# Seven query products of a cross-attention in another order, with one more accumulation bank and earlier bank copies

## The chip, the cores and the metric

The kernel runs on one NeuronCore of a Trainium2 chip. The metric is the device time of one execution in microseconds. Its engines are named as in the profile: PE (TensorE, matrix products), PEld (TensorE's weight loads), ACT (ScalarE), DVE (VectorE), POOL (GpSimd) and SP (SyncE, which here only issues transfers). Each engine works through its own queue in order; semaphores tie the queues together.

## The reference

One layer of a streaming encoder over 512 tokens with 1024 features, in fp32: a combined input projection, forgetting attention and a gated linear recurrence side by side, an output projection, cross-attention to 256 memory tokens, a squared-ReLU MLP, and a final norm. The change lies in the cross-attention:

```python
def memory_cross_attention(h, mem_n, w_q, w_kv, w_o):
    b_, s_, _ = h.shape
    m_ = mem_n.shape[1]
    q = (h @ w_q).reshape(b_, s_, X_HEADS, X_HEAD_DIM)
    kv = mem_n @ w_kv
    k, v = jnp.split(kv, 2, axis=-1)
    ...
    s = jnp.einsum('bshd,bmhd->bhsm', q, k).astype(jnp.float32) / math.sqrt(X_HEAD_DIM)
    p = jax.nn.softmax(s, axis=-1)
    o = jnp.einsum('bhsm,bmhd->bshd', p.astype(v.dtype), v).reshape(b_, s_, D_MODEL)
    return o @ w_o
```

There are four heads of 256 features. `h` is normalised before (its row scale is applied inside the softmax), and `w_q` is 1024 x 1024.

## The kernel before

**Precision.** Every fp32 operand of a large product is split into a high part that TensorE takes in one pass (dtype fp32r) and the rest as a low part. A product is then three matmuls: high x high, high x low and low x high. Splitting 128 x 1024 weights is one copy on ACT (line 190, `wh.. <- wr..`) and one subtraction on DVE (line 194, `wl.. <- wr..,wh..`). The raw weights come by transfers on SP's queue (line 216 for panels, line 322 for query products).

**Seven products.** For heads 2 and 3 (g = 1) the query product q = x @ w_q, with x cut into two halves of features and two halves of tokens, and w_q into two halves of features and two of columns, is not done as eight block products but as seven on sums of blocks, after Winograd's variant of Strassen's scheme. They are named 1 to 7; the sums of weight blocks (5, 6, 7) are made earlier by accumulating transfers into DRAM (`wsq`), the sums of activation blocks (5, 6, 3, 7) on ACT and DVE (`x1_sums`, line 1421 on; `x1_last` makes 3 in the buffers that 6 has used). Product 4's raw weights are those of product 6 plus a block that a transfer on POOL's queue adds in place, once product 6's weights are split (line 325).

Each product is 24 matmuls of 128 x 256 on two row blocks (lines 1485 to 1487). They are accumulated in PSUM banks: U takes products 1, 6, 7 and 4, one after the other. A copy of U after product 1 starts bank V, to which product 2 is added: this is head 2, tokens 0 to 255 (`xq..20`). Product 5 goes to bank Y and from there to SBUF (`y5s`, tile `xy`). A copy of U after product 6 replaces Y, to which product 3 is added. U after product 7 plus `y5s` is head 3, second half (`xt7`); U after product 4 is head 2, second half; Y after product 3 plus `y5s` is head 3, first half (`xt3`). `q_out` splits a result in high (`xqh`, ACT, line 1466) and low (`xql`, DVE, lines 1468 and 1470).

**Banks.** `mm(...)` takes a bank from a pool of three (`mmp`); a new tile takes a bank that is free first, and its first writer waits until all readers of the old tile are done. The weight parts rotate through four buffers each (`whp`, `wlp`), so a split waits until the matmuls on the buffer's previous weights are done.

**Order.** PE's order is that of the program text: `fill` is a list of generators, from which pieces are taken between the steps of the softmax of each head (`x_scores`: scores `xs`, maximum `xm`, exponent `xp` on ACT line 1528, division on DVE line 1531; `x_T_`: transposes `xpt`; `x_out`: outputs `xo`). ACT and DVE are ordered by a scheduler, by priority: text order, moved ahead by `ahead(n)` (`tc.high_priority`); weight splits are given out with `PW = -20`, bank copies with none. The lines that set it:

```python
    P1, P2, P3, P4, PW = 20, 20, 20, 10, -20
    ...
    QORDER = [(1, name) for name in "1256743"]
    ...
        if h == 1:
            for g, name in QORDER[:-1]:
                fill.add(q_product(g, name), f"q{g}{name}")
        if h == 2:
            fill.add(q_product(1, "3"), "q13")
    ...
        if h < 2:
            fill.until(("xq1", "q14")[h])
```

The order of the names in `QORDER` also sets the order in which their weights are loaded and split. After the second scores of head 1 a piece of this list runs up to the transposes of head 1; the rest, through product 4, runs before the outputs of head 1; product 3 runs among the scores of head 2.

Of the kernel before, what the change touches and what calls it, by code (L numbers as in the profile page):

```python
# [9 lines left out]
F32 = mybir.dt.float32  # L10
R = mybir.dt.float32r
U8 = mybir.dt.uint8
AF = mybir.ActivationFunctionType
ALU = mybir.AluOpType
AX = mybir.AxisListType

P = 128
# [4 lines left out]
M = 256  # L22
# [10 lines left out]
P1, P2, P3, P4, PW = 20, 20, 20, 10, -20  # L33
# [13 lines left out]
def emit(  # L47
# [22 lines left out]
    te, ve, ac, gp = nc.tensor, nc.vector, nc.scalar, nc.gpsimd  # L70
# [32 lines left out]
    def q2(name):  # L103
        return q2p.tile([P, S], R, tag="q2", name=name)
# [4 lines left out]
    def t2(name, dt=F32, shape=(S,)):  # L109
        return t2p.tile([P] + list(shape), dt, tag="t2", name=name)  # L110
# [6 lines left out]
    def mm(name, shape=(S,)):  # L117
        return mmp.tile([P] + list(shape), F32, tag="mm", name=name)
# [4 lines left out]
    def sc(name, shape=(S,)):  # L123
        return scp.tile([P] + list(shape), F32, tag="sc", name=name)
# [4 lines left out]
    def f(a):  # L129
        return a.bitcast(F32)  # L130


    def panel(w, n0):
        return [(slice(0, WT), w[:, n0 : n0 + WT].rearrange("(k p) n -> p k n", p=P))]
# [31 lines left out]
        specs.append(panel(w_out, j * WT))  # L166
    for j in range(2):
        specs.append(panel(w_xq, j * WT))
    QORDER = [(1, name) for name in "1256743"]
    QFIRST = len(specs)  # L170
    specs += [lambda g=g, n=n: q_unit(g, n) for g, n in QORDER]
    for j in range(4):
# [125 lines left out]
    def parts_of(i):  # L298
        return 1 if QFIRST <= i < QFIRST + len(QORDER) else 2

    q_raw = {}

    def q_unit(g, name):
        hi, lo = new_parts([UK, WT], f"q{g}{name}")
        stream.append(([hi], [lo]))
        if name == "4":
            raw = q_raw.pop(g)
        else:
            if name == "6":
                raw = q_raw[g] = s4([UK, WT], f"wrq{g}{name}")  # L310
            else:
                state["halves"] += 1
                if state["halves"] % 3 == 0:
                    raw = t4(f"wrq{g}{name}")
                else:
                    raw = wrp.tile([P, D], F32, tag="wr", name=f"wrq{g}{name}", padded_shape=[P, UK * UW])
                raw = raw.rearrange("p (k n) -> p k n", k=UK)
            if name in SUMS:
                src = wsum["q", g, name]
            else:  # L320
                src = block_q(g, {"1": "00", "2": "10", "3": "11"}[name])
            nc.sync.dma_start(raw, src)
        jobs = [split_of(hi, lo, raw)]
        if name == "6":
            jobs.append(lambda: tc.keep_in_program_order(gp.dma_start(raw, block_q(g, "10"), accum_op=ALU.add)))
        return jobs

    def next_panel():
        while len(stream) < len(specs) and sum(parts_of(i) for i in range(state["used"], len(stream) + 1)) <= 4:
            for split in load_next():  # L330
                with ahead(PW):
                    split()
        r = stream[state["used"]]
        state["used"] += 1
        return r
# [51 lines left out]
    def ahead(n):  # L387

        return tc.high_priority(offset=n) if n else nullcontext()
# [396 lines left out]
    for hp in range(2):  # L786
# [8 lines left out]
        for j in range(2):  # L795
            h = 2 * hp + j
            ps = mm(f"gq{h}")
# [52 lines left out]
    U, W = [], []  # L850
# [112 lines left out]
    for li, m in enumerate(mlev):  # L963
# [10 lines left out]
        for hp in range(2):  # L974
# [3 lines left out]
            ps = sc(f"lv{hp}{m}", (NT, 2, w))  # L978
# [305 lines left out]
    for n in range(len(pairs) + 2):  # L1284
        if n < len(pairs):
            p, tb = pairs[n]
# [120 lines left out]
    xq, xps, xpr, xpT = {h: {} for h in range(4)}, {}, {}, {}  # L1407
# [50 lines left out]
    qbank, y5s = {}, {}  # L1458

    def q_out(h, tp, src, sign):  # L1460
        def half(part):
            name = f"xq{part}{h}{tp}"
            return q2(name).rearrange("p (i n) -> p i n", i=2) if h % 2 == 0 else t2(name, R, (2, M))

        a, b = half("h"), half("l")
        ac.activation(a, src, AF.Copy, scale=sign)
        if sign > 0:
            ve.tensor_tensor(b, src, f(a), ALU.subtract)
        else:
            ve.scalar_tensor_tensor(b, src, sign, f(a), op0=ALU.mult, op1=ALU.subtract)  # L1470
        xq[h][tp] = [(a[:, i, :], b[:, i, :]) for i in range(2)]

    def q_product(g, name):
        b = {"5": "Y", "3": "Y", "2": "V"}.get(name, "U")
        if (g, b) not in qbank:
            qbank[g, b] = mm(f"xq{b}{g}").rearrange("p (i n) -> p i n", i=2)
            if b == "V":
                ac.activation(qbank[g, b], qbank[g, "U"], AF.Copy)
        ps = qbank[g, b]
        (whi,), (wlo,) = next_panel()  # L1480
        xh, xl = x1s[name]
        for k in range(UK):
            for i in range(2):
                ws, begin = slice(i * P, (i + 1) * P), name in "15" and k == 0 and i == 0
                te.matmul(ps[:, i, :], whi[:, k, ws], xh[:, k, :], start=begin, stop=False, skip_group_check=True)
                te.matmul(ps[:, i, :], whi[:, k, ws], xl[:, k, :], start=False, stop=False, skip_group_check=True)
                at = te.matmul(ps[:, i, :], wlo[:, k, ws], xh[:, k, :], start=False, stop=k == UK - 1, skip_group_check=True)
            yield presum.tick(6 * WT / 2400, at)
        if name == "2":
            q_out(2 * g, 0, ps, 1.0)  # L1490
        elif name == "4":
            q_out(2 * g, 1, ps, 1.0)
        elif name == "5":
            y5s[g] = t2(f"xy5{g}", F32, (2, M))
            ac.activation(y5s[g], ps, AF.Copy)
        elif name == "6":
            ac.activation(qbank[g, "Y"], ps, AF.Copy)
            x1_last()
        elif name in "73":
            t = t2(f"xt{name}{g}", F32, (2, M))  # L1500
            ve.tensor_tensor(t, ps, y5s[g], ALU.add)
            q_out(2 * g + 1, 1 if name == "7" else 0, t, -1.0)
# [73 lines left out]
    for h in range(4):  # L1576
# [5 lines that stand above are left out]
            x2_hi, x2_lo = act_tile("x2_hi"), act_tile("x2_lo")  # L1582
            early, rest = residual(o_hi, o_lo, g_ff, x2_hi, x2_lo, "xw", None, range(KC), 2, to_tok, first_hooks, True)
            fill.add(early())
        if h == 3:
            fill.until("q13")
        x_scores(h, 0)
        fill.run(X1)
        x_scores(h, 1)
        fill.run(X2 + X3)  # L1590
        x_T_(h, 0)
        x_T_(h, 1)
        pth, ptl = s4([2, S], f"pth{h}", R), s4([2, S], f"ptl{h}", R)
        for mc in range(2):
            ac.activation(pth[:, mc, :], xpT[h][mc], AF.Copy)
            ve.tensor_tensor(ptl[:, mc, :], xpT[h][mc], f(pth[:, mc, :]), ALU.subtract)
        if h < 2:
            fill.until(("xq1", "q14")[h])
        else:
            fill.run(X4)  # L1600
        x_out(h, pth, ptl)
# [599 lines left out]
```

## Time and profile before

| what | value |
|---|---|
| runs | 753.63, 755.44, 759.96 us (median 755.44) |
| profiled execution | 755.39 us |
| its span, first to last instruction | 753.6 us |
| mean granted clock of TensorE | 0.997 |
| products 1 (end) to 4 of heads 2 and 3 | 343.96 to 366.40 us in the span |

In the profile, times are in microseconds from the span's start. A timeline row gives start, duration, engine, line, operation, output <- inputs, size, and in brackets the idle time of the engine before it with the instruction that ended it (its releaser). The durations of matmuls overlap their successors, so distances between starts are what counts. A row of the view of waits reads: who waited <- for whom, total, times, longest. A row of the view of windows gives the stretch, its length, then the busy time of PE, PEld, DVE, ACT and POOL with counts of instructions, the granted clock of TensorE, the DMA share and GB/s. A row on transfers ends with the KB of each and the time from issue to landing.

### The profile page before, as it was taken

The numbers are of one execution on the slowest core, as the hardware profiler recorded it, in microseconds if no ns is written. First come the engines' busy times: TensorE is split into PE (matmuls) and PEld (weight loads), VectorE is DVE, ScalarE is ACT, GpSimd is POOL, SyncE is SP. The second block draws the span as 40 slices with busy tenths as digits, with TensorE's granted clock in tenths as the row PEclk, the third lists the DMA queues.
The fourth block names the chain that finished last, engine by engine and source line by source line (L and its number), as shares of the span: only waits on it lengthen the run. The fifth ranks groups of instructions, "written<-read, shape, count | busy, mean of one in ns | idle before, by whom it ended". The sixth has DMA issues, their size and how long they took to land.

```text
span 753.6 us, 12520 instructions
## 1 busy us (share of the span) xinstructions
PE 740.1 (98%) x4629; PEld 648.6 (86%) x4629; DVE 584.5 (78%) x918; ACT 470.8 (62%) x786; POOL 219.1 (29%) x294
## 2 busy tenths in 40 slices
PE   9999999999999999998899999999999999999996
PEld 6888888898888888888887899898989899998985
DVE  5877996677788867964656799978878787878796
ACT  5965776566666733444544589766675757574864
POOL 7225942442443347531111213111111111100024
PEclk9999999999999999999999999999999999999999
DMA  8787999847946999986857798989898998977452
GB/s 251 233 219 195 252 304 341 250 168 246 346 165 197 296 297 242 211 186 109 196 112 167 119 263 221 254 218 242 204 245 224 241 235 218 245 204 229 135 113 112
DMA packets 115263, 163.94 MB, mean 218 GB/s; under 512 B 6481, under 2 KB 76922, under 8 KB 115202
## 3 DMA queue, kind: packets, MB, share of 16 engines
q1 hardware_dynamic: 86978, 117.24, 47.4%
q0 software_dynamic: 28064, 45.64, 34.4%
q8 instruction: 36, 0.59, 0.3%
q10 hardware_dynamic: 160, 0.27, 0.1%
q14 instruction: 25, 0.20, 0.1%
HBM read 157.87 MB, written 54.54 MB: 282 GB/s over the span
## 4 chain that ended last, share of the span: by engine, by line
PE 88%; DMA 4%; DVE 4%; issue 2%; ACT 2%; POOL 0%; POOLq 0%; DVEq 0%; ACTq 0%; SPq 0%
PE uU L1776 4%; PE uU L1778 4%; PE uU L1777 4%; PE U L1934 4%; PE U L1935 4%; PE U L1936 4%; PE uY L1778 2%; PE uY L1777 2%; PE uY L1776 2%; PE xk L1189 2%; PE wo L352 2%; PE wo L354 2%; PE Y L1934 2%; PE Y L1936 2%; PE Y L1935 2%; PE wo L353 2%
## 5 line engine op out<-in xcount | busy, mean ns | idle before, releaser
L194 DVE TENSOR_TENSOR wlu<-wru,whu 128x1024 fp32r<-128x1024 f32 x53 | 63.9, 1221 | 25.8 <-ACT whu L190 25.6
L190 ACT ACTIVATE whu<-wru 128x1024 fp32r<-128x1024 f32 x53 | 55.7, 1059 | 41.5 <-PE U L1936 16.8
L194 DVE TENSOR_TENSOR wld<-wrd,whd 128x1024 fp32r<-128x1024 f32 x56 | 68.2, 1221 | 13.8 <-ACT whd L190 13.6
L190 ACT ACTIVATE whd<-wrd 128x1024 fp32r<-128x1024 f32 x56 | 59.0, 1054 | 14.6 <-PE uU L1777 7.2
L1934 PE MATMUL U<-whd,hb 128*128 128x512 f32 x120 | 46.8, 390 | 0.0
L1935 PE MATMUL U<-wld,hb 128*128 128x512 f32 x120 | 46.8, 390 | 0.0
L1936 PE MATMUL U<-whd,hb 128*128 128x512 f32 x120 | 46.7, 389 | 0.0
L1776 PE MATMUL uU<-xs_hi,whu 128*128 128x256 f32 x128 | 36.3, 284 | 0.0
L1778 PE MATMUL uU<-x_hi,wlu 128*128 128x256 f32 x128 | 36.2, 283 | 0.0
L1776 PE MATMUL uY<-xs_hi,whu 128*128 128x256 f32 x128 | 36.2, 283 | 0.0
L1777 PE MATMUL uY<-xs_lo,whu 128*128 128x256 f32 x128 | 36.2, 283 | 0.0
L1778 PE MATMUL uY<-xs_hi,wlu 128*128 128x256 f32 x128 | 36.2, 283 | 0.0
L1777 PE MATMUL uU<-x_lo,whu 128*128 128x256 f32 x128 | 36.2, 283 | 0.0
L1777 PE MATMUL uU<-xs_lo,whu 128*128 128x256 f32 x128 | 36.2, 283 | 0.0
L1778 PE MATMUL uU<-xs_hi,wlu 128*128 128x256 f32 x128 | 36.2, 283 | 0.0
L1776 PE MATMUL uU<-x_hi,whu 128*128 128x256 f32 x128 | 36.2, 283 | 0.0
L1210 POOL TENSOR_SCALAR bi<-nF,Ft 128x128 f32<-128x128 f32 (+3 forms) x32 | 20.5, 649 | 52.4 <-PE pt L1246 30.9
L1672 POOL DMA_DIRECT2D wrd<-in_w_dram x8 | 9.7, 1213 | 83.4 <-DVE wld L194 76.3
L551 POOL DMA_DIRECT2D wsd<-in_w_dram x16 | 17.4, 1089 | 55.0 <-PE xw L354 13.4
L1672 POOL DMA_DIRECT2D wru<-in_w_dram x7 | 9.2, 1320 | 80.0 <-DVE wlu L194 80.0
L551 POOL DMA_DIRECT2D wsu<-in_w_dram x14 | 17.6, 1257 | 41.5 <-PE xw L354 18.5
L1936 PEld LDWEIGHTS U<-whd,hb 128*128 128x128 f32 x120 | 22.5, 188 | 4.8
(1028 smaller groups left out, 2726.3 us busy)
## 6 DMA issues: line engine op xcount, KB each, us to landing
wru<-in_w_dram SPq DMA_DIRECT2D x25, 512.0 KB, 6.2
wsd<-in_w_dram SPq DMA_DIRECT2D x24, 512.0 KB, 7.3
wrd<-in_w_dram SPq DMA_DIRECT2D x24, 512.0 KB, 8.0
wrd<-wsd SPq DMA_DIRECT2D x24, 512.0 KB, 4.2
wsu<-in_w_dram SPq DMA_DIRECT2D x21, 512.0 KB, 7.0
wru<-wsu SPq DMA_DIRECT2D x21, 512.0 KB, 4.8
wsd<-in_w_dram POOLq DMA_DIRECT2D x16, 512.0 KB, 7.6
wsu<-in_w_dram POOLq DMA_DIRECT2D x14, 512.0 KB, 7.8
```

The source lines that it names most:

```text
L190: at = ac.activation(hi, raw, AF.Copy)
L194: at_lo = ve.tensor_tensor(lo, raw, f(hi), ALU.subtract)
L352: te.matmul(ps, wh, hi, start=n_ == 0 and not begun, stop=False)
L551: yield gp.dma_start(wsum[kind, g, name], src, accum_op=ALU.add, **more)
L1210: gp.tensor_scalar(bi[:, 0:n], fF[h][:, 0:n], -1.0, Ft[:, tb, h : h + 1], op0=ALU.mult, op1=ALU.add)
L1672: tc.keep_in_program_order(gp.dma_start(box[0], block(g, "10"), accum_op=ALU.add))
L1776: te.matmul(ps[:, i, :], whi[:, k, ws], xh[:, k, :], start=begin, stop=False, skip_group_check=True)
L1777: te.matmul(ps[:, i, :], whi[:, k, ws], xl[:, k, :], start=False, stop=False, skip_group_check=True)
L1778: at = te.matmul(ps[:, i, :], wlo[:, k, ws], xh[:, k, :], start=False, stop=k == UK - 1, skip_group_check=True)
L1934: te.matmul(ps, hi, whi[:, k, :], start=begin, stop=False, skip_group_check=True)
L1935: te.matmul(ps, hi, wlo[:, k, :], start=False, stop=False, skip_group_check=True)
L1936: at = te.matmul(ps, lo, whi[:, k, :], start=False, stop=k == 1, skip_group_check=True)
```

## The change

The seven products run in the order 1, 5, 6, 2, 7, 4, 3 in place of 1, 2, 5, 6, 7, 4, 3. The copy of U that starts V is given out right behind product 1, with priority `P1`, and not when product 2 begins; the copy of U into Y gets the same priority. Product 4 starts a bank Z of its own (its first matmul overwrites); its result is put together from a copy of U in SBUF (`xt4`, a new activation) and an addition on DVE (new).

```diff
-    QORDER = [(1, name) for name in "1256743"]
+    QORDER = [(1, name) for name in "1562743"]
...
     def q_product(g, name):
-        b = {"5": "Y", "3": "Y", "2": "V"}.get(name, "U")
-        if (g, b) not in qbank:
-            qbank[g, b] = mm(f"xq{b}{g}").rearrange("p (i n) -> p i n", i=2)
-            if b == "V":
-                ac.activation(qbank[g, b], qbank[g, "U"], AF.Copy)
-        ps = qbank[g, b]
+        b = {"5": "Y", "3": "Y", "2": "V", "4": "Z"}.get(name, "U")
+
+        def bank(b):
+            qbank[b] = mm(f"xq{b}{g}").rearrange("p (i n) -> p i n", i=2)
+
+        if b not in qbank:
+            bank(b)
+        ps = qbank[b]
         (whi,), (wlo,) = next_panel()
         xh, xl = x1s[name]
         for k in range(UK):
             for i in range(2):
-                ws, begin = slice(i * P, (i + 1) * P), name in "15" and k == 0 and i == 0
+                ws, begin = slice(i * P, (i + 1) * P), name in "154" and k == 0 and i == 0
...
             yield presum.tick(6 * WT / 2400, at)
-        if name == "2":
+        if name == "1":
+            bank("V")
+            with ahead(P1):
+                ac.activation(qbank["V"], ps, AF.Copy)
+        elif name == "2":
             q_out(2 * g, 0, ps, 1.0)
         elif name == "4":
-            q_out(2 * g, 1, ps, 1.0)
+            t = t2(f"xt4{g}", F32, (2, M))
+            ac.activation(t, qbank["U"], AF.Copy)
+            ve.tensor_tensor(t, ps, t, ALU.add)
+            q_out(2 * g, 1, t, 1.0)
         elif name == "5":
             y5s[g] = t2(f"xy5{g}", F32, (2, M))
             ac.activation(y5s[g], ps, AF.Copy)
         elif name == "6":
-            ac.activation(qbank[g, "Y"], ps, AF.Copy)
+            with ahead(P1):
+                ac.activation(qbank["Y"], ps, AF.Copy)
             x1_last()
```

PE has the same instructions; the products stand in the new order, and the eight transposes of head 1 (`xpt1`) stand behind product 5, where they stood behind product 2. What the scheduler made of ACT and DVE is read from the built programs. In the names, the two digits of a query product's tiles are g and the product (`whq17`: high part of the weights of product 7); in `xp11`, `xs11` and `pth1` they are head and half of the tokens.

ACT, around the end of product 1, before:

```order
L190 ACTIVATE whq16_3923<-wrq16_3925 128x1024
L1551 ACTIVATE o_hi_3631<-xo0_3874 128x512
L1551 ACTIVATE o_hi_3631<-xo1_3883 128x512
L1528 ACTIVATE xp10_3910,xd10_3909<-xs10_3892,xn10_3907,r0_435 128x256 x2
L190 ACTIVATE whq17_3980<-wrq17_3982 128x1024
L1528 ACTIVATE xp11_3966,xd11_3965<-xs11_3948,xn11_3963,r0_435 128x256 x2
L1478 ACTIVATE xqV1_3978<-xqU1_3916 128x512
L190 ACTIVATE whq14_4032<-wrq16_3925 128x1024
```

ACT, the same place, in the change:

```order
L190 ACTIVATE whq16_3917<-wrq16_3919 128x1024
L1561 ACTIVATE o_hi_3631<-xo0_3874 128x512
L190 ACTIVATE whq12_3924<-wrq12_3926 128x1024
L1561 ACTIVATE o_hi_3631<-xo1_3883 128x512
L1538 ACTIVATE xp10_3910,xd10_3909<-xs10_3892,xn10_3907,r0_435 128x256 x2
L190 ACTIVATE whq17_3981<-wrq17_3983 128x1024
L1494 ACTIVATE xqV1_3978<-xqU1_3916 128x512
L1538 ACTIVATE xp11_3966,xd11_3965<-xs11_3948,xn11_3963,r0_435 128x256 x2
L190 ACTIVATE whq14_4030<-wrq16_3919 128x1024
```

The copy into V moved ahead of one softmax step, and stays behind the split of product 7. The split of product 2 now stands between the two output copies; the split of product 5 took its earlier place.

ACT, from the split of product 4 on, before:

```order
L190 ACTIVATE whq14_4032<-wrq16_3925 128x1024
L1466 ACTIVATE xqh20_4027<-xqV1_3978 128x512
L1595 ACTIVATE pth1_4021<-xpt10_4011 128x512
L1595 ACTIVATE pth1_4021<-xpt11_4012 128x512
L190 ACTIVATE whq13_4062<-wrq13_4064 128x1024
L1495 ACTIVATE xy51_4060<-xqY1_4031 128x512
L190 ACTIVATE wh38a_4130<-wr38a_4132 128x1024
L1497 ACTIVATE xqY1_4031<-xqU1_3916 128x512
L1425 ACTIVATE o_hi_3631<-xdif_3469 128x1024
```

ACT, the same place, in the change:

```order
L190 ACTIVATE whq14_4030<-wrq16_3919 128x1024
L1504 ACTIVATE xy51_4028<-xqY1_3980 128x512
L1605 ACTIVATE pth1_4022<-xpt10_4012 128x512
L1605 ACTIVATE pth1_4022<-xpt11_4013 128x512
L190 ACTIVATE whq13_4065<-wrq13_4067 128x1024
L1507 ACTIVATE xqY1_3980<-xqU1_3916 128x512
L1425 ACTIVATE o_hi_3631<-xdif_3469 128x1024
L190 ACTIVATE wh38a_4131<-wr38a_4133 128x1024
L1466 ACTIVATE xqh20_4096<-xqV1_3978 128x512
L190 ACTIVATE wh38b_4135<-wr38b_4137 128x1024
L1466 ACTIVATE xqh31_4126<-xt71_4124 128x512
L1499 ACTIVATE xt41_4168<-xqU1_3916 128x512
```

The copy into Y stands behind the split of product 3, and ahead of that of the first output panel (`wh38a`); V's high half (`xqh20`) moved behind both. The last row is the new copy.

DVE, at product 7, in the change (before, the low half `xql20` stood directly ahead of product 3's `wlq13`, and there was no `xt41`):

```order
L194 TENSOR_TENSOR wlq13_4066<-wrq13_4067,whq13_4065 128x1024
L1429 SCALAR_TENSOR_TENSOR o_lo_3632<-xdif_3469,o_hi_3631 128x1024
L194 TENSOR_TENSOR wl38a_4132<-wr38a_4133,wh38a_4131 128x1024
L1468 TENSOR_TENSOR xql20_4097<-xqV1_3978,xqh20_4096 128x512
L1511 TENSOR_TENSOR xt71_4124<-xqU1_3916,xy51_4028 128x512
L194 TENSOR_TENSOR wl38b_4136<-wr38b_4137,wh38b_4135 128x1024
L1470 SCALAR_TENSOR_TENSOR xql31_4127<-xt71_4124,xqh31_4126 128x512
L1500 TENSOR_TENSOR xt41_4168<-xqZ1_4130,xt41_4168 128x512
```

The low half of V, its last reader, moved behind two weight steps. In the built program Z has V's bank, and product 4's first matmul waits for DVE there. On SP's queue the loads of `wrq12` and `wrq15` change places; POOL's queue has the same order.

## The prediction

> **What bounds the kernel now.** I read the page first: busy time by engine and the chain that ended last.
>
> ```profile
> span 753.6 us, 12520 instructions
> PE 740.1 (98%) x4629; PEld 648.6 (86%) x4629; DVE 584.5 (78%) x918; ACT 470.8 (62%) x786; POOL 219.1 (29%) x294
> PE 88%; DMA 4%; DVE 4%; issue 2%; ACT 2%; POOL 0%; POOLq 0%; DVEq 0%; ACTq 0%; SPq 0%
> ```
>
> TensorE (PE) is busy for 98% of the span, so only two things can be won: moments when it waits, and moments when its clock is low. The view of waits, cut to PE, orders the first kind.
>
> ```profile
> PE xqV L1485 <- ACT xqV L1478: 2.6, 1, 2.6
> PE xqU L1485 <- ACT xqY L1497: 1.5, 1, 1.5
> PE warm L464 <- DVE ones L468: 1.3, 1, 1.3
> PE xqU L1485 <- DVE xt L1501: 0.8, 1, 0.8
> ```
>
> Three of the four longest waits lie in the seven query products of heads 2 and 3, which are what the change reorders. The timeline of PE there (start, duration, and in brackets the idle time before, with its releaser) gives their real price.
>
> ```profile
> 343.84 0.28 PE L1487 MATMUL xqU<-x_hi,wlq 128*128 128x256 f32 x1
> 346.73 0.47 PE L1485 MATMUL xqV<-x_hi,whq 128*128 128x256 f32 x1 [2.61 <-ACT xqV L1478]
> 351.20 1.03 PE L1540 MATMUL xpt<-ident,xp 128*128 128x128 f32 x8
> 352.00 0.36 PE L1485 MATMUL xqY<-o_hi,whq 128*128 128x256 f32 x1
> 354.94 0.28 PE L1485 MATMUL xqU<-o_hi,whq 128*128 128x256 f32 x1
> 357.70 0.28 PE L1487 MATMUL xqU<-o_hi,wlq 128*128 128x256 f32 x1
> 359.50 0.39 PE L1485 MATMUL xqU<-o_hi,whq 128*128 128x256 f32 x1 [1.51 <-ACT xqY L1497]
> 362.36 0.28 PE L1487 MATMUL xqU<-o_hi,wlq 128*128 128x256 f32 x1
> 363.42 0.39 PE L1485 MATMUL xqU<-x_hi,whq 128*128 128x256 f32 x1 [0.78 <-DVE xt L1501]
> 366.40 0.40 PE L1548 MATMUL xo<-pth,xvh 128*128 128x512 f32 x1
> ```
>
> Matmuls overlap, so I go by starts. A product is 24 matmuls; product 6, undisturbed, runs from 354.94 to 357.82 (its last start, 357.70, and one step of 0.12): 2.88 us. Against that, PE loses 2.77 us before product 2 (343.96 to 346.73), 1.68 us before product 7 (357.82 to 359.50) and 0.94 us before product 4 (362.48 to 363.42). And product 2 itself takes 346.73 to 351.20, 4.47 us, 1.59 more than it should. The windows say why (the columns that matter: length, PE busy, and the granted clock, third from the right).
>
> ```profile
> 346.73:350.30 3.57, 3.57 (x17) 3.57 (x18) 0.35 (x2) 0.00 (x0) 0.00 (x0) 0.52 0.44 149
> 350.30:357.82 7.52, 7.52 (x65) 7.48 (x64) 4.25 (x5) 4.07 (x6) 1.91 (x2) 1.00 0.44 70
> 359.50:363.42 3.92, 3.14 (x25) 2.94 (x25) 2.64 (x3) 1.79 (x2) 0.00 (x0) 1.00 1.09 238
> 400.00:746.00 346.00, 346.00 (x2180) 314.44 (x2179) 286.48 (x359) 232.78 (x334) 57.55 (x56) 1.00 0.82 206
> ```
>
> After the 2.6 us gap the clock is 0.52 for 3.57 us; after the 1.5 us gap it stays at 1.00. The last row matters for what follows: from 400 to 746 us PE has no idle time at all, so time saved here is not taken up by a later wait that already exists.
>
> **What goes.** The four losses add up to 2.77 + 1.59 + 1.68 + 0.94 = 6.98 us. Whether they go depends on ScalarE (ACT), a queue in which a waiting instruction holds back all behind it, and then on VectorE (DVE).
>
> ```profile
> 338.41 0.60 ACT L1551 ACTIVATE o_hi<-xo 128x512 fp32r<-128x512 f32 x1 [0.63 <-PE xo L1550]
> 344.04 1.06 ACT L190 ACTIVATE whq<-wrq 128x1024 fp32r<-128x1024 f32 x1 [2.01 <-PE xqU L1486]
> 345.01 0.55 ACT L1528 ACTIVATE xp<-xs,xn,r 128x256 f32<-128x256 f32 x1
> 346.00 0.20 ACT L1528 ACTIVATION_READ_ACCUMULATOR xp<-xs,xn,r 128x1 f32 x1
> 346.09 0.59 ACT L1478 ACTIVATE xqV<-xqU 128x512 f32<-128x512 f32 x1
> 351.28 1.06 ACT L190 ACTIVATE whq<-wrq 128x1024 fp32r<-128x1024 f32 x1 [4.60 <-PE xqV L1486]
> 352.73 1.08 ACT L1595 ACTIVATE pth<-xpt 128x512 fp32r<-128x512 f32 x2
> 357.90 1.06 ACT L190 ACTIVATE wh38a<-wr38a 128x1024 fp32r<-128x1024 f32 x1 [1.34 <-PE xqU L1486]
> 358.87 0.58 ACT L1497 ACTIVATE xqY<-xqU 128x512 f32<-128x512 f32 x1
> 346.47 0.62 DVE L1531 TENSOR_SCALAR xp<-xp,xd 128x256 f32<-128x256 f32 x2
> 354.72 0.68 DVE L1468 TENSOR_TENSOR xql<-xqV,xqh 128x512 fp32r<-128x512 f32 x1
> 358.99 1.23 DVE L194 TENSOR_TENSOR wl38a<-wr38a,wh38a 128x1024 fp32r<-128x1024 f32 x1 [1.65 <-ACT wh38a L190]
> ```
>
> Each bank copy comes late because a weight split (1.06 us, line 190) stands ahead of it and itself waits for PE to free its buffer: V's copy ends at 346.68 behind the split of product 7 and four pieces of softmax, Y's at 359.45 behind that of wh38a.
>
> The V copy: moved ahead of the second pair of softmax pieces (345.01 to 346.20), but not ahead of the split at 344.04, it now runs from about 345.0 to 345.55. Product 2 starts two products later, so this loss goes with its cold clock: 4.36. Product 5, now next, waits for nothing late (its weights are split where product 2's were).
>
> The Y copy: it is queued behind the split of product 3, which needs product 6's buffer. Product 6 runs to about 350.8, so the split ends near 351.9 and the copy near 352.45. Product 7 comes only after product 2, at about 353.7. The 1.68 goes, with 1.2 us to spare; the cover is product 2.
>
> The read of U: product 4 now writes Z, so it no longer waits for the addition on DVE: the 0.94 goes. But there are only three such banks, and Z takes the one of V, so product 4 waits for V's last reader instead.
>
> **What comes.** First, the transposes of head 1's probabilities. They stood 4.47 + 2.77 us behind product 1, and now stand 2.88 behind it, at 346.84. The probabilities end later than before, because the copy (0.59, 0.50 in step) went ahead of their softmax: DVE's scaling, 346.47 to 347.09 before, moves to about 346.97 to 347.59. The first four transposes take 0.4 (eight take 351.20 to 352.00), the last two begin at about 347.65 and the eighth ends near 347.9 in place of 347.64: 0.3 us. The split of product 2, which now stands between the two o_hi copies (338.41), makes the first half of the softmax 1.0 us later too, but that has 3 us of slack. Bounds: nothing, if the copy runs in a gap, to 0.3 + 1.06 if one more split gets between.
>
> Second, product 4 on V's bank. On ACT, wh38a's split waits for the end of product 2 (353.7) and runs to 354.8, the copy of V takes 0.58 to 355.3; on DVE the split of wl38a (1.23) ends at 356.1 and the low half of V (0.68) at 356.8. Product 7 ends at 353.7 + 2.88 = 356.6. So 0.3 us with the wake-up. Bounds: nothing to the 0.94 of the wait it replaces, which is the nearest row.
>
> Third, the new work: a copy of U into SBUF on ACT (0.58, as the copy of Y) and an addition on DVE (as the low halves, 0.68). Nobody waits: the result is used by the second scores of head 2, and between lie the outputs of head 1 (12 matmuls), the first scores (12) and 18 matmuls of product 3, over 6 us. Zero, and up to about 0.7 if the copy's chain were late. The SP queue swaps the loads of products 2 and 5, both long before use: zero. POOL's queue keeps its order.
>
> The sum: 6.98 - 0.3 - 0.3 = 6.4 us saved. The profiled execution took 755.39 (span 753.6 and 1.8 around it), within 0.05 of the median of the runs, 755.44. So 749.0. With the bounds, 6.98 - 1.36 - 0.94 = 4.7 to 6.98: 748.4 to 750.7.
>
> [...]
>
> **Rivals.** (a) Another queue wait takes the place of those removed: both copies still stand behind splits, and if the split of product 2 or 4 slips by its own 1.06 us the transposes and product 7 both pay, with the 0.94 kept at Z. Gain 6.98 - 1.36 - 0.94 - 1.06 = 3.6: 751.8. For it: the copies passed none of the splits. Against: 1.2 us of slack at Y. Chance 0.10.
>
> (b) The slow stretch is not the gap's and stays: 749.0 + 1.59 = 750.6. Against it: it begins with the first matmul after the gap, and the two shorter gaps show 1.00. [...] Chance 0.05.
>
> (c) The end is slower than before. The split of product 4 now heads ACT's queue from 346.7 and waits for a transfer of its own:
>
> ```profile
> 338.85 1.33 POOL L325 DMA_DIRECT2D wrq<-in_w_xq_dram  x1 [1.99 <-DVE wlq L194]
> wrq<-in_w_xq_dram POOLq DMA_DIRECT2D x1, 512.0 KB, 8.9
> ```
>
> Issued at 338.85 and 8.9 us under way, it lands at 347.75; before, that split ran only at 351.28 and saw nothing of it. Behind it queue y5's copy, the two pth copies (1.08), product 3's split and Y's copy, 4.3 us in all, so a landing after 349.4 delays product 7, microsecond for microsecond, and past 2.6 us of idle the cold 1.59 returns. It decides the sign from a landing at 349.4 + 4.8 = 354.2, 15.4 us after the issue; at 362, it is slower by 1%: about 763. For it: wr38a's load now falls into the same stretch. Chance 0.04.
>
> (d) The priorities do nothing: V passes only one softmax step and Y none. That changes little, since the order of the products covers both copies, and without V's move the 0.3 at the transposes would go: 748.7, inside the forecast's range.
>
> (e) The gain is lost later to the weight stream (DMA share 0.82 from 400 on): 755. Against: no PE wait there. Chance 0.04.
>
> **How the numbers follow.** The forecast, with (d), has 0.77: 749.0. 1% of 755.44 is 7.55, about what a measurement of this kernel can tell from no change; the line is 747.9. The ceiling of 6.98 does not reach it, only run-to-run spread does (the three runs lie between 753.63 and 759.96, the lowest 1.8 below the median): 0.25 for faster. Slower by over 1% is (c) at its end and a bad spread: 0.05. The rest, 0.70, lies within 1%. The range goes down to 747.0 (ceiling and a low run) and up to 752.5, to take in (a) and (b).
>
> **What would show it.** In the profile after: no wait of PE on xqV or on the Y copy; granted clock 1.00 throughout from 344 to 361; wait of the transposes on xp about 0.3 and of xqZ on xql about 0.3; the outputs of head 1 starting near 360.0 in place of 366.40. Wrong would be: a wait of product 7 on ACT, a cold stretch, or new PE waits after 400.

## The result: 748.70 us, and the profile after

| what | before | after |
|---|---|---|
| median of the runs | 755.47 us (6 runs, 753.63 to 759.96) | 748.70 us (6 runs, 748.28 to 750.03) |
| ratio | | 0.9907, 95% interval 0.9881 to 0.9934 |
| profiled execution, its span | 755.39, 753.6 us | 750.03, 748.3 us |
| end of product 1 to head 1's first outputs | 343.96 to 366.40: 22.44 us | 345.19 to 361.04: 15.85 us |

Faster by 0.9%, the forecast (749.0) being 0.3 us off. The page after the change, its span, its busy times and its chain of work:

```profile
span 748.3 us, 12523 instructions
PE 738.5 (99%) x4629; PEld 647.1 (86%) x4629; DVE 582.5 (78%) x919; ACT 470.9 (63%) x787; POOL 218.0 (29%) x294
PE 93%; DVE 2%; issue 2%; ACT 1%; DMA 1%; SPq 0%; POOL 0%; POOLq 0%; DVEq 0%; ACTq 0%
```

PE's part of the chain went from 88 to 93%. The view of waits, cut to PE, has lost its three rows of the query products:

```profile
PE pk L1098 <- ACT A L1061: 1.6, 1, 1.6
PE warm L464 <- DVE ones L468: 1.3, 1, 1.3
PE xpt L1550 <- DVE xp L1541: 0.5, 1, 0.5
PE xw L353 <- DVE o_lo L1562: 0.2, 1, 0.2
```

The first row belongs to another stage, some 220 us earlier, where before had waited 0.5 us. It makes this one execution some 1.1 us longer, and it comes and goes: the second profile of the same kernel (the run a1_again below, span 746.9 us) doesn't have it, and a kernel in the old order (d1_gap2) has 1.3 us of it. It is also most of why this profile stands later: product 1 ends 1.23 us later than before. So the piece, and not the span of one profile, is what I compare.

PE's timeline after the change, the last matmul of product 1 and then the first one of each step:

```profile
345.07 0.28 PE L1489 MATMUL xqU<-x_hi,wlq 128*128 128x256 f32 x1
345.19 0.28 PE L1487 MATMUL xqY<-o_hi,whq 128*128 128x256 f32 x1
348.07 1.29 PE L1550 MATMUL xpt<-ident,xp 128*128 128x128 f32 x8
349.11 0.36 PE L1487 MATMUL xqU<-o_hi,whq 128*128 128x256 f32 x1
352.07 0.28 PE L1487 MATMUL xqV<-x_hi,whq 128*128 128x256 f32 x1
354.95 0.28 PE L1487 MATMUL xqU<-o_hi,whq 128*128 128x256 f32 x1
357.71 0.28 PE L1489 MATMUL xqU<-o_hi,wlq 128*128 128x256 f32 x1
358.10 0.35 PE L1487 MATMUL xqZ<-x_hi,whq 128*128 128x256 f32 x1
361.04 0.40 PE L1558 MATMUL xo<-pth,xvh 128*128 128x512 f32 x1
```

Products 5, 6, 2, 7 and 4 follow each other almost without a break: 2.88, 2.96, 2.88, 2.88 and 2.94 us, with 1.04 us from the first transpose to product 6 and 0.27 us (357.83 to 358.10) ahead of product 4. The windows (length, then the busy times; the granted clock is third from the right) of the piece, and of the rest of the kernel:

```profile
343.80:361.00 17.20, 17.09 (x141) 16.63 (x141) 12.85 (x19) 11.72 (x20) 2.92 (x3) 1.00 0.79 180
400.00:741.00 341.00, 341.00 (x2155) 310.34 (x2154) 282.35 (x354) 229.04 (x328) 56.90 (x56) 1.00 0.83 209
```

The clock is 1.00 throughout, and behind 400 us PE still has no idle time. From the first outputs of head 1 to the end it is 753.6 - 366.40 = 387.20 us before and 748.3 - 361.04 = 387.26 after: what the piece saved, 6.59 us, was kept to the end.

ACT's timeline shows how the copies now lie:

```profile
345.27 1.06 ACT L190 ACTIVATE whq<-wrq 128x1024 fp32r<-128x1024 f32 x1 [1.06 <-PE xqU L1488]
346.23 0.58 ACT L1494 ACTIVATE xqV<-xqU 128x512 f32<-128x512 f32 x1
348.15 1.06 ACT L190 ACTIVATE whq<-wrq 128x1024 fp32r<-128x1024 f32 x1 [0.22 <-PE xqY L1488]
352.20 1.06 ACT L190 ACTIVATE whq<-wrq 128x1024 fp32r<-128x1024 f32 x1 [1.53 <-issue]
353.16 0.58 ACT L1507 ACTIVATE xqY<-xqU 128x512 f32<-128x512 f32 x1
355.03 1.06 ACT L190 ACTIVATE wh38a<-wr38a 128x1024 fp32r<-128x1024 f32 x1 [0.31 <-PE xqV L1488]
355.99 0.58 ACT L1466 ACTIVATE xqh<-xqV 128x512 fp32r<-128x512 f32 x1
```

Both copies still stand behind a split (at 345.27 and at 352.20). V's copy ends at 346.81, but product 2 wants it only at 352.07; Y's ends at 353.74, 1.2 us ahead of product 7 at 354.95. The waits did not get shorter, they moved under other products.

### The profile page after: what moved, and what is told of

Same layout as the page of the kernel before. It is cut to its first block, busy times and chain, and to the rows that moved or that the text cites. A ratio compares the mean times of both kernels' runs of the same rounds, so it can differ in the third digit from the quotient of the medians.

```text
span 748.3 us, 12523 instructions
## 1 busy us (share of the span) xinstructions
PE 738.5 (99%) x4629; PEld 647.1 (86%) x4629; DVE 582.5 (78%) x919; ACT 470.9 (63%) x787; POOL 218.0 (29%) x294
## 4 chain that ended last, share of the span: by engine, by line
PE 93%; DVE 2%; issue 2%; ACT 1%; DMA 1%; SPq 0%; POOL 0%; POOLq 0%; DVEq 0%; ACTq 0%
PE uU L1786 4%; PE uU L1788 4%; PE uU L1787 4%; PE U L1945 3%; PE U L1944 3%; PE U L1946 3%; PE uY L1788 2%; PE uY L1787 2%; PE uY L1786 2%; PE xk L1189 2%; PE wo L352 2%; PE wo L353 2%; PE wo L354 2%; PE xw L353 2%; PE xw L354 2%; PE xw L352 2%
```

## The experiments

In all of them I read the piece from the end of product 1 (its last matmul's start and one step of 0.12) to the first output of head 1: 22.44 us before, 15.85 after. The first four kernels are the parts of the change; the kernel before, on the same chip, took 754.59 us (19 runs).

**The order alone (e1_order).** Into the kernel before, the new order; V's copy must then go out behind product 1, since product 6 adds to U before product 2 runs. No priority, and product 4 in U as before.

```diff
-    QORDER = [(1, name) for name in "1256743"]
+    QORDER = [(1, name) for name in "1562743"]
...
-            if b == "V":
-                ac.activation(qbank[g, b], qbank[g, "U"], AF.Copy)
...
+        if name == "1":
+            qbank[g, "V"] = mm(f"xqV{g}").rearrange("p (i n) -> p i n", i=2)
+            ac.activation(qbank[g, "V"], ps, AF.Copy)
```

> The new order of the products alone: V's copy stands right behind product 1 in the text, but without priority, so ACT makes it after head 1's second softmax step; product 4 is added in U as before. If the order is what saves the time: no wait of TensorE on V or Y and no cold stretch, the 0.94 us before product 4 stays, no wait at the transposes. From the last matmul of product 1 to head 1's outputs 16.2 us (before 22.44, after 15.85), time about 749.1. If the priorities or bank Z carry it: 18 to 22 us in that piece, 752 to 755.

Measured: 748.51 us (4 runs), ratio 0.9921 (0.9904 to 0.9937). The timeline of PE has one wait left in the piece, the old one of product 4:

```profile
343.83 0.28 PE L1483 MATMUL xqY<-o_hi,whq 128*128 128x256 f32 x1
346.71 1.04 PE L1541 MATMUL xpt<-ident,xp 128*128 128x128 f32 x8
347.50 0.36 PE L1483 MATMUL xqU<-o_hi,whq 128*128 128x256 f32 x1
357.15 0.39 PE L1483 MATMUL xqU<-x_hi,whq 128*128 128x256 f32 x1 [0.78 <-DVE xt L1502]
360.12 0.40 PE L1549 MATMUL xo<-pth,xvh 128*128 128x512 f32 x1
```

343.83 to 360.12 is 16.29 us: 6.15 of the 6.59 us come from the order with the V copy it forces.

**The bank alone (e2_bankz).** Old order, old copies, product 4 in Z.

```diff
-        b = {"5": "Y", "3": "Y", "2": "V"}.get(name, "U")
+        b = {"5": "Y", "3": "Y", "2": "V", "4": "Z"}.get(name, "U")
...
-            q_out(2 * g, 1, ps, 1.0)
+            t = t2(f"xt4{g}", F32, (2, M))
+            ac.activation(t, qbank[g, "U"], AF.Copy)
+            ve.tensor_tensor(t, ps, t, ALU.add)
+            q_out(2 * g, 1, t, 1.0)
```

> Bank Z alone, in the old order. By the terms of the sum only the wait of product 4 on the addition goes, since V's readers are long done: 21.5 us in the piece (before 22.44), time 754.5, which is no change that times can show. If Z carried more of the gain, the piece would be under 20.

Measured: 753.96 us (10 runs), ratio 0.9991 (0.9982 to 1.0). The wait of product 4 is gone, those of 2.61 and 1.51 us are not, and the piece takes 21.41 us: 1.03 less, the 0.94 of the wait and 0.1 that a product takes longer when it starts behind one (2.98 us against 2.88). In the new order the bank brings less: there product 4 waits 0.27 us on V's bank in place of 0.94 on U (16.29 us in e1_order, 15.59 in e4_noprio below, which is that kernel with the bank: 0.70).

**The copies alone (e3_copies).** Old order, both copies early and with priority, product 4 in U.

```diff
-            if b == "V":
-                ac.activation(qbank[g, b], qbank[g, "U"], AF.Copy)
...
+        if name == "1":
+            qbank[g, "V"] = mm(f"xqV{g}").rearrange("p (i n) -> p i n", i=2)
+            with ahead(P1):
+                ac.activation(qbank[g, "V"], ps, AF.Copy)
...
+            with ahead(P1):
+                ac.activation(qbank[g, "Y"], ps, AF.Copy)
```

> The earlier copies with priority alone, in the old order. V's copy passes one softmax step, so the gap before product 2 shrinks from 2.77 to about 1.7 us; Y's copy stays where it was, its 1.68 remains. If the cold stretch is the gap's: clock 1.00 in product 2, 19.8 us in the piece, time 752.8. If it has another cause: 0.52 again for 3.6 us, 21.4 us, 754.4.

Measured: 752.84 us (10 runs), ratio 0.9977 (0.9968 to 0.9986); piece 19.85 us. This run parts the two explanations of the slow clock. In PE's timeline the wait of product 2 has shrunk to 1.51 us, and with it the slow stretch has gone: product 2 takes 345.51 to 348.49, 2.98 us in place of 4.47. The Y wait is what it was, priority or not.

```profile
345.51 0.39 PE L1483 MATMUL xqV<-x_hi,whq 128*128 128x256 f32 x1 [1.51 <-ACT xqV L1490]
348.49 1.04 PE L1543 MATMUL xpt<-ident,xp 128*128 128x128 f32 x8
356.79 0.39 PE L1483 MATMUL xqU<-o_hi,whq 128*128 128x256 f32 x1 [1.51 <-ACT xqY L1500]
360.71 0.39 PE L1483 MATMUL xqU<-x_hi,whq 128*128 128x256 f32 x1 [0.78 <-DVE xt L1504]
```

**Without the priorities (e4_noprio).** The changed kernel, both `with ahead(P1):` taken away.

```diff
-            with ahead(P1):
-                ac.activation(qbank["V"], ps, AF.Copy)
+            ac.activation(qbank["V"], ps, AF.Copy)
...
-            with ahead(P1):
-                ac.activation(qbank["Y"], ps, AF.Copy)
+            ac.activation(qbank["Y"], ps, AF.Copy)
```

> The change without its two priorities. If V's earlier copy does nothing but delay head 1's softmax: the wait of the transposes on DVE (0.28 us after) goes, the one of product 4 on V's last reader (0.3) stays, 15.6 us in the piece (after 15.85), time 748.4, the same as after. If the priorities matter for the gain: a wait of TensorE on V or Y comes back and the piece is 17 us or more.

Measured: 748.40 us (4 runs), ratio 0.9923 (0.9908 to 0.9938); piece 15.59 us, 0.26 less than with them. The whole difference lies at the transposes, which product 6 now follows after 0.79 us (1.04 with the priorities):

```profile
347.02 1.04 PE L1548 MATMUL xpt<-ident,xp 128*128 128x128 f32 x8
347.81 0.36 PE L1487 MATMUL xqU<-o_hi,whq 128*128 128x256 f32 x1
356.78 0.36 PE L1487 MATMUL xqZ<-x_hi,whq 128*128 128x256 f32 x1
```

Y's copy keeps its place on ACT without its priority; V's goes behind the softmax piece it had passed. So in the new order the priority on V's copy costs a quarter of a microsecond and brings none.

**How long a wait it takes for the slow clock (d1_gap2, d2_gap3, d4_gap5).** The kernel of e3_copies with V's copy made two, three and five times over, which lengthens PE's idle time ahead of product 2 and nothing else of what PE does. (The kernel before took 755.59 us beside these; one execution each.)

```diff
-                ac.activation(qbank[g, "V"], ps, AF.Copy)
+                for _ in range(2):
+                    ac.activation(qbank[g, "V"], ps, AF.Copy)
```

> The kernel of e3_copies (old order, early copies; TensorE idle 1.51 us ahead of product 2, which then ran at full clock in 2.98 us) with V's copy made twice in a row on ScalarE, to the same bank. Each further copy should add some 0.52 us, so an idle stretch near 2.0 us. Theory (idle time above a bound that lies somewhere between 1.68 us, which stayed at full clock, and 2.61 us, which did not, costs a slow stretch): open, 2.0 lies between them; product 2 takes 2.98 us if it is under the bound and about 4.3 to 4.5 us if over. Rival (the bound is above 3 us, and the slow stretch of before has another cause): 2.98 us, time 753.4. With a slow stretch the time is about 754.9.

> As d1_gap2 with V's copy made three times: idle stretch near 2.55 us, about the 2.61 us of the kernel before. Theory: granted clock about 0.52 for some 3.5 us behind the gap, product 2 takes about 4.4 us in place of 2.98, time about 755.4. Rival (bound above 3 us): product 2 stays at 2.98 us, time 753.9.

> As d1_gap2 with V's copy made five times: idle stretch near 3.6 us. Theory with a price that does not depend on the length of the idle time: product 2 takes about 4.4 us as behind 2.61 us, time about 756.5. Theory with a price that grows with it: the slow stretch is longer than 3.57 us, product 2 over 4.6 us, time above 756.8. The rival with a bound above 3 us expects a slow stretch here too, so this run only gives the price.

The idle times came out longer than I had worked out, because ACT put one piece of softmax (d1_gap2) or two (the other kernels), 0.54 us each, between the copies: 2.57, 3.62 and 4.85 us. So the 2.0 us that d1_gap2 was built for were not tried by it. The runs took 756.24, 756.18 and 757.41 us. The last is above the 756.8 us that was named for a growing price, but only because the idle time came out 1.2 us longer than worked out; product 2 itself took 4.47 us, and not over 4.6. The first matmul of product 2, then the first transpose, in PE's timeline of d1_gap2:

```profile
347.72 0.58 PE L1483 MATMUL xqV<-x_hi,whq 128*128 128x256 f32 x1 [2.57 <-ACT xqV L1491]
352.15 1.04 PE L1544 MATMUL xpt<-ident,xp 128*128 128x128 f32 x8
```

The windows of d4_gap5, the idle time and what follows:

```profile
343.90:348.73 4.83, 0.00 (x1) 0.00 (x1) 2.17 (x5) 4.71 (x10) 0.00 (x0) 1.00 0.72 156
348.73:352.20 3.47, 3.47 (x16) 3.47 (x17) 0.00 (x0) 0.00 (x0) 0.00 (x0) 0.52 0.09 32
352.20:353.20 1.00, 1.00 (x9) 1.00 (x9) 0.00 (x0) 0.00 (x0) 0.24 (x1) 0.95 0.00 0
```

All waits of this length in the piece, over all profiles, with the time of the product that begins behind them (undisturbed: 2.98 us behind a wait):

| idle time of PE | in | the product behind it takes |
|---|---|---|
| 1.51 to 1.52 us | before, e2, d1, d2, d4 (at Y), e3 (at V and at Y) | 2.98 us, seven times of seven |
| 2.07 us | t1_late (at Y) | 4.47 us |
| 2.57 to 2.61 us | before, e2, d1 (at V) | 4.47, 4.29, 4.43 us |
| 3.62 us | d2 (at V) | 4.28 us |
| 4.85 us | d4 (at V) | 4.47 us |

In these profiles the clock stayed at 1.00 behind waits of 1.51 and 1.52 us, and a slow stretch came with each of the waits of 2.07 to 4.85 us; a wait of 1.56 us in another stage of the changed kernel (the row `pk` above, at 125.73) left it at 1.00 too. No wait between 1.56 and 2.07 us was measured. The price, 1.3 to 1.5 us, didn't grow with the idle time. The rival that set the bound above 3 us falls by d1_gap2, and so does the theory of a growing price.

**A late transfer (t1_late).** Rival (c) as a measured thing: the changed kernel without priorities, in which the accumulating transfer for product 4's weights may be issued only when V's copy is done.

```diff
-            jobs.append(lambda: tc.keep_in_program_order(gp.dma_start(raw, block_q(g, "10"), accum_op=ALU.add)))
+            late_acc.append(lambda: gp.dma_start(raw, block_q(g, "10"), accum_op=ALU.add))
...
-            ac.activation(qbank["V"], ps, AF.Copy)
+            at = ac.activation(qbank["V"], ps, AF.Copy)
+            dma = late_acc.pop()()
...
+            tc.add_manual_dep(dma.ins, at.ins.name, sync, reason="late transfer")
...
```

> The changed kernel without its two priorities (e4_noprio: 748.40 us, piece 15.59 us), with the accumulating transfer that product 4's weights wait for issued only when V's copy is done, some 6 us later than there. The order of ScalarE then has the split of product 4 behind the two copies of the transposed probabilities, and behind it product 3's split and Y's copy. Rival (c) of the prediction, as a model of the queue: free until a landing about 2.9 us ahead of product 7's start (near 350.8), then microsecond for microsecond. With 6.6 us under way the landing is near 352.5: product 7 starts 1.7 us later, time about 750.2; with 8.9 us under way, landing near 354.8: 4.0 us later and a slow stretch of 1.6 us on top, time about 754.0. In both the wait of TensorE stands at product 7's first matmul and is put down to Y's copy. The other theory (there is enough slack in the queue for the transfer): piece 15.6 us, time 748.4.

Measured: 752.39 us (5 runs), ratio 0.9951 (0.9932 to 0.997); piece 19.08 us. The rows of POOL, ACT and PE, in order:

```profile
347.31 1.33 POOL L325 DMA_DIRECT2D wrq<-in_w_xq_dram  x1 [10.12 <-DVE xp L1543]
353.49 2.00 ACT L190 ACTIVATE whq<-wrq 128x1024 fp32r<-128x1024 f32 x2 [4.26 <-DMA wrq<-in_w_xq_dram]
355.40 0.58 ACT L1509 ACTIVATE xqY<-xqU 128x512 f32<-128x512 f32 x1
356.03 0.49 PE L1487 MATMUL xqU<-o_hi,whq 128*128 128x256 f32 x1 [2.07 <-ACT xqY L1509]
360.50 0.28 PE L1487 MATMUL xqZ<-x_hi,whq 128*128 128x256 f32 x1
```

The transfer, issued 8.3 us later than in e4_noprio (there at 339.02), lands just before 353.49 and holds the two splits and Y's copy behind it; product 7 starts at 356.03, 2.23 us after product 2's end at 353.80, and then takes 4.47 us. 2.23 for the queue and 1.59 for product 7 (1.49 of it the slow clock, 0.10 the restart behind a wait), less the 0.26 for which product 4 no longer waits and the 0.07 of its own restart: 3.49, and 19.08 - 15.59 = 3.49 is measured. The time lies between the two that were expected, 750.2 and 754.0: the transfer was issued 8.3 us later and not some 6, and the slow stretch, which had been counted only behind a wait of 4.0 us, came behind 2.07. The model of the queue holds, with 2.5 us from the landing to product 7 where 2.9 had been worked out, and so does its warning that the slow stretch returns, though from a shorter wait than the prediction said. Even so the kernel stays faster than before.

**A version with none of the new waits (e5_best), and the changed kernel again (a1_again).** e4_noprio with ACT's order held at one place: product 2's high half (`xqh20`) before the split of panel 38a. Both kernels ran on one chip; the kernel before took 754.77 us there.

```diff
-                    split()
+                    at = split()
+                if "q2h" in q2h:
...
+                    tc.add_manual_dep(at.ins, q2h.pop("q2h").ins.name, order_only, reason="product 2 first")
...
-        ac.activation(a, src, AF.Copy, scale=sign)
+        at = ac.activation(a, src, AF.Copy, scale=sign)
+        if (h, tp) == (2, 0):
+            q2h["q2h"] = at
```

> The changed kernel without its two priorities, and with ScalarE's order held so that the high half of product 2's result is taken before the split of the panel behind product 3 (38a) and not behind it. Theory: the 0.3 us for which product 4 waits comes from VectorE's second read of V's bank, which stands behind that split and its low half; the read then ends about 1.1 us before product 4 is due, its wait is gone, the piece from product 1's end to head 1's first outputs takes 15.3 us (15.85 in the changed kernel, 15.59 without the priorities), and the time is about 0.3 us below the version without priorities, 0.5 below the changed kernel: 748.1 to 748.3. Rival (the wait has another source, such as the change of banks itself): product 4 still starts 0.38 us behind product 7's last matmul, piece 15.6 us.

> The changed kernel once more, on the chip and beside the runs of e5_best: 748.7 us, piece 15.85 us with the waits of 0.3 us at the transposes and 0.3 us at product 4; the wait of 1.6 us at the first projections of the other stage (PE pk), which made its profiled run 1.2 us longer than its other runs, is expected at about 0.5 us here.

Measured: e5_best 748.48 us (5 runs, 748.02 to 749.14), ratio 0.9917 (0.9903 to 0.9931), piece 15.26 us; a1_again 748.33 us (4 runs, 747.88 to 748.75), ratio 0.9915 (0.9901 to 0.9929), piece 15.85 us. The last read of V's bank ends at 357.95 in the changed kernel, 0.15 us ahead of product 4's start (358.10); in e5_best it ends at 355.33, and product 4 starts at 356.59:

```profile
357.26 0.69 DVE L1468 TENSOR_TENSOR xql<-xqV,xqh 128x512 fp32r<-128x512 f32 x1
354.65 0.68 DVE L1473 TENSOR_TENSOR xql<-xqV,xqh 128x512 fp32r<-128x512 f32 x1
```

The windows of e5_best show PE busy through the whole piece, and product 4 follows product 7 by a plain step:

```profile
344.21:359.47 15.26, 15.26 (x131) 15.26 (x130) 11.64 (x16) 11.29 (x18) 2.96 (x3) 1.00 0.78 183
```

That confirms where the 0.27 us came from (a split and its low half ahead of the last read of V), and the piece is 0.59 us shorter, 0.26 of it by leaving out the priorities and 0.33 by the order on ACT. The time isn't: 748.48 against 748.33, above the 748.1 to 748.3 that were expected, and the runs of one kernel lie some 1 us apart. What is left to gain in this piece is below what these runs can measure.

## Why the prediction was right, point by point

- **The V gap, 2.77, and its slow clock, 1.59.** Both went. That the second is the gap's, and not the place's, is shown by e3_copies (shorter gap, old order, full clock) and by d1_gap2 (gap as long as before, slow again). Rival (b) falls. The size was a little off: at full clock a product behind a wait took 2.98 us (seven times in the table above), not 2.88, so 1.49 of the 1.59 is the clock and 0.10 the restart. The slow clock did not come in at the same place in every kernel: 0.16 us behind the first matmul in before, and between 0.44 us ahead of it and 1.26 us behind it in the others (the table of the last section).
- **The Y gap, 1.68.** Went by the cover that was named, product 2, with the 1.2 us to spare that were forecast. e3_copies shows that the priority has no part in it: in the old order the Y wait stayed at 1.51.
- **Product 4's wait for U, 0.94, against Z's for V, 0.3.** The wait went, and 0.27 came, behind the split of wh38a and its low half as worked out; e5_best took these away and the wait with them.
- **The transposes, 0.3.** 0.24 more than before (1.04 against 0.80), and e4_noprio shows it to be the priority's.
- **The new copy and addition at zero.** No instruction of PE waits for them; the new addition stands at 361.31 on DVE.
- **The sum.** Forecast 6.4 us, measured 6.59 in the trace, 6.77 between the medians and 6.44 in the second comparison (a1_again). The terms: waits 5.39 down to 0.27, products 16.25 down to 14.54, transposes 0.80 up to 1.04. Of the 0.2 us missing in the forecast, 0.12 is in the products other than product 2, for which I had priced nothing: product 7 takes 0.10 less without a wait ahead of it and product 4 0.04 less, while 5 and 6 nearly cancel; the rest are the two new waits, each a little under 0.3. The outputs of head 1 start at 361.04, and not near 360.0, because the piece itself starts 1.23 us later in this profile.
- **Rival (a)** didn't come: neither split slipped by its 1.06 us, and the slack at Y was there. **Rival (d)** is true as told: in the new order the priorities bring nothing. **Rival (e)** didn't come: 387.2 us from head 1's outputs to the end, before and after.
- **Rival (c)** didn't come: the transfer, issued at 340.07, took 6.6 us, and its split, at 348.15, was released by the end of product 5, not by the transfer. t1_late shows the mechanism to be real. One number in it was wrong: in t1_late the slow stretch returned behind a wait of 2.07 us, and not only past 2.6.

The largest chance, 0.70, was put on a change within 1%; the 0.93% measured lie inside, but close to that line, as the ceiling of 6.98 had said.

## What to carry to other kernels

A copy that is late because its engine's queue is full of splits need not be made earlier: putting a product that doesn't need it in between was worth 6.15 us here, and the priorities on top of it nothing (in the old order the earlier copies alone brought 2.59 us). Price a wait of TensorE with the clock behind it: here a wait of 1.5 us cost 1.8 us in all (1.68 between the starts and 0.10 of restart) and one of 2.1 us cost 3.8 (2.23 and 1.59), so between these two, 0.56 us less of idle time were worth some 2.0 us. And a bank from a small pool traded one wait for another here (0.94 us on U for 0.27 on V's bank); look up whose bank it takes and what its last reader is queued behind.

## What the runs showed of the hardware

In all six kernels that have a slow stretch in the piece it was 3.41 to 3.42 us long, and it did not begin with the first matmul. The traces keep the times at which the granted clock changed; a window of the profile laid from one change to the next reads 0.50. The window of the same length ahead of it, and then the slow stretch itself, in before and in e2_bankz (the second number is PE's busy time, the granted clock is third from the right):

```profile
343.48:346.89 3.41, 0.80 (x7) 0.60 (x6) 2.54 (x6) 2.64 (x6) 0.00 (x0) 1.00 0.90 144
346.89:350.30 3.41, 3.41 (x17) 3.41 (x18) 0.19 (x1) 0.00 (x0) 0.00 (x0) 0.50 0.46 156
344.13:347.54 3.41, 1.26 (x10) 1.26 (x11) 1.92 (x4) 2.10 (x6) 0.00 (x0) 1.00 0.73 110
347.54:350.96 3.42, 3.42 (x18) 3.42 (x17) 0.00 (x0) 0.36 (x1) 0.93 (x1) 0.50 0.40 138
```

The six kernels, in the order of PE's idle time in the 3.41 us ahead of the slow stretch:

| kernel | wait | idle time of PE in the 3.41 us ahead | the slow stretch begins |
|---|---|---|---|
| t1_late (at Y) | 2.07 us | 2.07 us | 0.13 us behind the first matmul |
| e2_bankz (at V) | 2.61 us | 2.15 us | 1.26 us behind it |
| d1_gap2 (at V) | 2.57 us | 2.50 us | 0.07 us ahead of it |
| before (at V) | 2.61 us | 2.61 us | 0.16 us behind it |
| d2_gap3 (at V) | 3.62 us | 3.18 us | 0.44 us ahead of it |
| d4_gap5 (at V) | 4.85 us | 3.26 us | 0.16 us behind it |

In e3_copies, with 1.51 us of idle time at V, there is none: 1.00 from 345.51 to 348.49. What sets the start of a slow stretch, and how short a wait can bring one, was not shown.

Where the slow stretch lay accounts for the differences in price. In e2_bankz it reaches into the transposes, which begin at 350.57, so product 2 alone looks cheaper there (4.29 us), but product 2 and the transposes together cost the same 1.5 us more (4.29 and 0.99 us, against 2.98 and 0.80 undisturbed); in d2_gap3 0.44 us of the slow stretch lie in the idle time, and the price is 1.30.

Not every execution of the kernel before seems to have had the slow stretch: of the 35 that ran beside the experiments, five read a mean granted clock of 0.999 or 1.000, though 3.41 us at 0.50 take 0.0023 off the mean over a span of 753.6 us. So, as an estimate from these clocks, the 1.49 us of the slow clock are probably lost in most executions of the kernel before, and not in all. The one profile of it that was kept has the slow stretch.
